# A hybrid block on one core: two weight sums of a pooling unit move to VectorE, its passes stand behind low parts, early branch weights, and the pooling weights' loads ahead of head 0's v

## The chip, the core and the metric

One core of one Trainium2 chip runs the whole kernel. The metric is the device time of one execution in microseconds (us). The kernel before takes 889.95 us, the median of three runs between 889.82 and 890.5. All times below are from one profiled execution of it, unless the text says otherwise.

## The reference, cut to what matters

One layer on 512 tokens of width 1024: a norm, one wide projection whose columns feed three mixers and the branch gates, the three branches merged by sigmoid gates, an output projection, and a feed-forward part. The change sits where the projection's pooling columns and the third branch's gate columns are computed, and where the pooling mixer and the first attention head begin.

```python
h = rms_norm(x, norm_mix[l])
proj = jnp.einsum('bsd,dc->bsc', h, w_in[l])
u_pool, u_lru, q, k, v, g_logits = jnp.split(proj, splits, axis=-1)
gates = jax.nn.sigmoid(g_logits + b_gate[l]).reshape(B, S, N_BRANCH, D_MODEL)
...
for g, w in enumerate(POOL_WINDOWS):            # windows 2, 4, 8, 16
    ug = u32[..., g * POOL_GROUP:(g + 1) * POOL_GROUP]
    cs = jnp.cumsum(ug, axis=1)
    cs_lag = jnp.pad(cs, ((0, 0), (w, 0), (0, 0)))[:, :S]
    outs.append((cs - cs_lag) / jnp.minimum(pos, float(w)) - ug)
y_pool = jnp.einsum('bsgi,gij->bsgj', jnp.stack(outs, axis=2), w_pool) * pool_scale
...
merged = (gates[:, :, 0] * jnp.einsum('bsc,cd->bsd', y_pool, w_branch[l, 0])
          + gates[:, :, 1] * jnp.einsum('bsc,cd->bsd', y_lru, w_branch[l, 1])
          + gates[:, :, 2] * jnp.einsum('bsc,cd->bsd', y_sb, w_branch[l, 2]))
```

## The kernel before, in words

Every product runs in float32 as three matmuls: each operand is split into a high part (rounded to fp32r) and a low part (the rest), and high by high, high by low and low by high are added in PSUM. `split_w` (L136) splits a weight tile of 128x1024: ScalarE writes the high part `whi` (L142), VectorE the low part `wlo` (L143). Both come from a pool of three buffers, so the split for product n+3 waits until TensorE is done with product n.

Q, k and v, the pooling columns and the gate columns of the third branch use a seven-product scheme: a square of four weight blocks 11, 12, 21, 22 is multiplied with seven products, named 11, 12, S1, S2, S3, S4, 22, whose weights are sums of blocks. The sums are built in place. A load on SyncE's queue brings a block, and a DMA on GpSimd's queue adds another block to it (`accum_op=ALU.add`, "an adding DMA" below), or VectorE adds two tiles. `pool_load` (L239) loads the pooling blocks and adds 22 to 21 (L244); `add_pool7` (L246) splits, and then starts the next sum with an adding DMA (L251). `seven_load` (L189) and `add_seven` (L200) do the same for the gate blocks (L196, L198), with two sums on VectorE (L207, L212) and one adding DMA (L213).

The stage concerned runs from 248.8 us on: 14 products for two pooling units in the order `PORDER` (L231), then 14 for two gate units (3 and 4) in `ORDER` or `UORDER`. Each product is 24 matmuls of 256 columns (`product`, L336, L342). The pooling units' PSUM tiles are `ps_uy`, `ps_ux`, the gate units' `ps_gy`, `ps_gx`. A product's half of a PSUM tile is used again by a later one, so ScalarE first copies it out: "a snap", L957 into `u` (pooling), L985 into `gx`, `gy` (gates). When a tile is complete, VectorE adds it to its snap (L962, L921). Then `pool_mean` (L927) makes the windowed mean of each half of `u` on VectorE: one pass per window, a running sum (L937) with a short one for the first columns (L936), or a shifted add (L934) for window 2, and two more operations (L939, L941). For the gates, `gate_done` (L919) takes the sigmoid (L923) and stores the tile to DRAM over GpSimd's queue (L925).

Behind the gates come head 0's transposes `pq` (L1102), the first branch product `ps_br` with the lru output loaded back as `yHH`, `yHL` over GpSimd's queue (L1250), the scores `z` of head 0 in three tiles from a pool of two PSUM buffers (`scores`, L1116), and the pooling map `pps` (`pool_back`, L1057). ScalarE reads `z` twice (L1135 writes `K`, L1136 writes `A`), which frees its PSUM buffer. The pooling weights `rawp` are loaded over SyncE's queue (L1045) and split by ScalarE (L1047, `wph`) and VectorE (L1048). `q_scales` (L842) makes the row scales of q on GpSimd, and its first operation is a power (L369).

The order of each engine's instructions is fixed when the kernel is built: a scheduler follows the program's order and the priorities (`high_priority`, `issue_after`). Each engine and each queue then works through its list in that order, and an instruction that waits holds up all behind it.

## Time and profile before

| | us |
|---|---|
| median of three runs | 889.95 |
| the profiled execution's own time | 890.54 |
| its span, first to last instruction | 888.8 |
| TensorE busy in the span | 863.5 |
| VectorE, ScalarE, GpSimd busy | 744.7, 528.2, 96.7 |

The profile is of one execution. Its page lists the busy time of each engine (PE is TensorE, DVE is VectorE, ACT is ScalarE, POOL is GpSimd, SP is SyncE). The view of waits says what TensorE stood idle for. The chain of waits follows the work that ended last. The table by stretch gives busy time, number of instructions, granted clock of TensorE (PEclk, 1.00 is full) and DMA share. A row of the timeline has start, duration, engine, line and tiles, and in brackets the idle time of the engine ahead of it with what ended it.

### The profile page before, as it was taken

To read this page: it belongs to the slowest core of one execution; us is meant where nothing else is said; L and a number is where in the kernel's file an instruction comes from. 1 tells how busy PE (TensorE), PEld (TensorE's weight loads), DVE (VectorE), ACT (ScalarE), POOL (GpSimd) and SP (SyncE) were. 2 spreads that over 40 slices of the span, in tenths; PEclk is the share of its full clock that TensorE was granted. 3 is DMA by queue.
4 is the path that set the end of the run, shared out by engine and by line. 5 is a ranking of instruction groups with operands and counts; after the bars stand their busy time and mean duration, and the time that the engine had idled before them with its cause. 6 is when DMAs were issued, how large, how long until landed. Compare 5 with 4: busy or idle time off the path is not lost.

```text
span 888.8 us, 14571 instructions
## 1 busy us (share of the span) xinstructions
PE 863.5 (97%) x5707; PEld 794.9 (89%) x5707; DVE 744.7 (84%) x947; ACT 528.2 (59%) x733; POOL 96.7 (11%) x139
## 2 busy tenths in 40 slices
PE   9999999999989896999999999999999999999998
PEld 7888878888879895888988998889999999999998
DVE  6899898979766964897998696699988898898974
ACT  7555998667844364676655554545555555754642
POOL 1010002232360021000000200000000000121200
PEclk9999999999999999999999999999999999999999
DMA  9685365997799358754554975437353343788923
GB/s 341 168 302 162 96 205 151 286 266 229 251 252 255 72 167 282 211 159 147 193 146 91 204 184 186 128 99 199 111 139 109 96 119 102 233 209 210 195 51 119
DMA packets 114757, 158.31 MB, mean 178 GB/s; under 512 B 8320, under 2 KB 86144, under 8 KB 114688
## 3 DMA queue, kind: packets, MB, share of 16 engines
q1 hardware_dynamic: 100864, 107.30, 38.0%
q0 software_dynamic: 13680, 49.81, 24.5%
q8 instruction: 45, 0.74, 0.4%
q10 hardware_dynamic: 144, 0.26, 0.1%
q14 instruction: 24, 0.20, 0.1%
HBM read 136.90 MB, written 18.87 MB: 175 GB/s over the span
## 4 chain that ended last, share of the span: by engine, by line
PE 80%; ACT 6%; DVE 6%; DMA 4%; issue 2%; POOL 1%; SPq 0%; DVEq 0%; ACTq 0%; POOLq 0%
PE ps_y L342 11%; PE ps_x L342 8%; PE ps_q L858 7%; PE ps_dy L1710 5%; PE ps_dx L1710 4%; PE ps_br L334 3%; PE ps_br L335 3%; PE ps_br L333 3%; PE ps_bY L1334 2%; PE ps_gate L761 2%; PE ps_gy L342 2%; DMA pw<-in_w_pool_dram 2%; PE ps_bX L1334 2%; DVE wlo L143 2%; ACT whi L142 1%
## 5 line engine op out<-in xcount | busy, mean ns | idle before, releaser
L142 ACT ACTIVATE whi<-raw 128x1024 fp32r<-128x1024 f32 x61 | 64.3, 1054 | 64.9 <-PE ps_out L334 15.3
L143 DVE TENSOR_TENSOR wlo<-raw,whi 128x1024 fp32r<-128x1024 f32 x61 | 74.3, 1220 | 15.9 <-ACT whi L142 15.5
L142 ACT ACTIVATE whi<-qw 128x1024 fp32r<-128x1024 f32 x48 | 50.4, 1053 | 33.8 <-PE ps_q L858 11.9
L143 DVE TENSOR_TENSOR wlo<-qw,whi 128x1024 fp32r<-128x1024 f32 x48 | 58.3, 1219 | 13.7 <-ACT whi L142 13.7
L1495 ACT ACTIVATE wh_S<-w_S 128x1024 fp32r<-128x1024 f32 x36 | 38.4, 1066 | 28.9 <-PE ps_y L342 20.3
L1616 POOL DMA_DIRECT2D dw<-in_w_down_dram x20 | 17.4, 971 | 306.1 <-DMA dw<-in_w_down_dram 253.6
L1496 DVE TENSOR_TENSOR wl_S<-w_S,wh_S 128x1024 fp32r<-128x1024 f32 x36 | 43.8, 1219 | 3.3 <-ACT wh_S L1495 3.3
L1495 ACT ACTIVATE wh<-w 128x1024 fp32r<-128x1024 f32 x27 | 28.7, 1063 | 27.5 <-PE ps_x L342 9.4
L1496 DVE TENSOR_TENSOR wl<-w,wh 128x1024 fp32r<-128x1024 f32 x27 | 32.9, 1219 | 7.8 <-ACT wh L1495 7.8
L1495 ACT ACTIVATE whdS<-dw 128x1024 fp32r<-128x1024 f32 x20 | 21.2, 1061 | 20.1 <-PE ps_dy L1710 10.6
L143 DVE TENSOR_TENSOR wlo<-pw,whi 128x1024 fp32r<-128x1024 f32 x14 | 17.1, 1221 | 16.5 <-ACT whi L142 16.4
L1496 DVE TENSOR_TENSOR wldS<-dw,whdS 128x1024 fp32r<-128x1024 f32 x20 | 24.1, 1219 | 4.9 <-ACT whdS L1495 4.9
L142 ACT ACTIVATE whi<-pw 128x1024 fp32r<-128x1024 f32 x14 | 14.8, 1059 | 21.9 <-DMA pw<-in_w_pool_dram 14.1
L1139 DVE TENSOR_TENSOR_SCAN E<-K,ahead 128x512 f32<-128x512 f32 (+3 forms) x32 | 25.3, 812 | 1.1 <-ACT K L1135 1.0
L333 PE MATMUL ps_br<-yHH,whi 128*128 128x512 f32 x64 | 25.2, 394 | 0.5 <-DVE gy L921 0.5
L334 PE MATMUL ps_br<-yHL,whi 128*128 128x512 f32 x64 | 25.2, 394 | 0.0
L335 PE MATMUL ps_br<-yHH,wlo 128*128 128x512 f32 x64 | 24.8, 387 | 0.0
L333 PE MATMUL ps_lru<-HH,whi 128*128 128x512 f32 x64 | 24.6, 384 | 0.0
L333 PE MATMUL ps_br<-yph,whi 128*128 128x512 f32 x64 | 24.5, 383 | 0.0
L333 PE MATMUL ps_gate<-HH,whi 128*128 128x512 f32 x64 | 24.4, 381 | 0.0
L335 PE MATMUL ps_lru<-HH,wlo 128*128 128x512 f32 x64 | 24.3, 379 | 0.0
L334 PE MATMUL ps_lru<-HL,whi 128*128 128x512 f32 x64 | 24.3, 379 | 0.0
(778 smaller groups left out, 3557.2 us busy)
## 6 DMA issues: line engine op xcount, KB each, us to landing
qw<-in_w_qkv_dram SPq DMA_DIRECT2D x24, 512.0 KB, 7.1
raw<-in_w_in_dram SPq DMA_DIRECT2D x23, 512.0 KB, 5.1
dw<-in_w_down_dram POOLq DMA_DIRECT2D x20, 512.0 KB, 8.6
w<-in_w_ffn_gate_dram SPq DMA_DIRECT2D x36, 256.0 KB, 4.1
w<-in_w_ffn_up_dram SPq DMA_DIRECT2D x36, 256.0 KB, 4.1
raw<-in_w_branch_dram SPq DMA_DIRECT2D x16, 512.0 KB, 4.1
qw<-in_w_qkv_dram POOLq DMA_DIRECT2D x12, 512.0 KB, 8.2
qd<-r POOLq DMA_DIRECT2D x12, 512.0 KB, 7.2
```

Of the source, the lines that this page charges most:

```text
L142: act(hi, raw, AF.Copy)
L143: los.append(dve.tensor_tensor(lo, raw, hi.bitcast(F32), ALU.subtract).ins)
L333: nc.tensor.matmul(ps, lh, rh, start=start, stop=False, skip_group_check=skip)
L334: nc.tensor.matmul(ps, lh, rl, start=False, stop=False, skip_group_check=skip)
L335: nc.tensor.matmul(ps, ll, rh, start=False, stop=stop, skip_group_check=skip)
L342: nc.tensor.matmul(o, a_[a][:, w, k, :], il2(b_[b][:, k, :]), start=first and n == k == 0, stop=last and n == 2 and k == 3, skip_group_che ...
L858: nc.tensor.matmul(ps[:, a, :], b_[:, k, ts_], il(a_[:, kk, :]), start=first and n == k == 0, stop=n == 2 and k == 3, skip_group_check=True)
L1139: dve.tensor_tensor_scan(E[:, c0:c0 + n][:, ::-1], K[:, c0 + 1:c0 + n + 1][:, ::-1], ahead[:, S - n:][:, ::-1], 0.0, ALU.mult, ALU.add)
L1334: nc.tensor.matmul(o, ah[x_][:, w, k, :], il2(b[k][y_]), start=first_ and n == k == 0, stop=n == 2 and k == 3, skip_group_check=True)
L1495: act(h, src, AF.Copy)
L1496: dve.tensor_tensor(l, src, h.bitcast(F32), ALU.subtract)
L1710: nc.tensor.matmul(o, a_[a][:, w, k0 + k, :], il2(b_[b][:, k, :]), start=first and i == k == 0, stop=last and i == 2 and k == nk - 1, skip ...
```

## The change

Six edits, all between the pooling units and head 0:

1. Pooling unit 0: the weights of S2 and S4 are sums made on VectorE, in place of two adding DMAs. One adding DMA (for S3) is left. Unit 1 keeps its three.
2. `PORDER` has another order.
3. `pool_mean` does one pass a call and is called behind given products (`MEAN` for unit 0, in gate unit 4 for unit 1), each pass placed behind the latest low part; it was one entry of the list of background work for two passes.
4. Gate unit 4 uses `ORDER` like unit 3 (S3 ahead of S4); `UORDER` is gone.
5. Three branch weight tiles are called for in gate unit 3 (`load_early`), and `q_scales` stands behind the last adding DMA of pooling unit 1.
6. The four `rawp` tiles are taken first and their loads stand ahead of head 0's v; the loads of head 0's q and k are called where its tasks are made.

```diff
     def add_direct(key, src, a, b):
-        def make(n):
+        def load(n):
             raw = wp.tile([P, a, b], F32, tag="raw", name="raw" + n)
             raws.append(nc.sync.dma_start(raw, src).ins)
-            return split_w(raw, [P, a, b], n)
+            return raw
+
+        def make(n):
+            return split_w(early.pop(key, None) or load(n), [P, a, b], n)
...
-    UORDER = {4: ("11", "12", "S2", "S1", "S4", "S3", "22")}
...
-    PORDER = ((0, "11"), (0, "S1"), (1, "11"), (1, "S1"), (0, "S2"), (0, "12"), (0, "S3"), (1, "S2"),
-              (0, "S4"), (0, "22"), (1, "12"), (1, "S3"), (1, "S4"), (1, "22"))
+    PORDER = ((0, "11"), (0, "S1"), (1, "11"), (0, "S2"), (0, "12"), (0, "S3"), (1, "S1"), (0, "S4"),
+              (0, "22"), (1, "S2"), (1, "12"), (1, "S3"), (1, "S4"), (1, "22"))
...
     def add_pool7(u, nm):
         def make(n):
-            parts = split_w(praw[u, {"S1": "21", "S2": "21", "S3": "11", "S4": "21"}.get(nm, nm)], [P, 2, 4, P], n)
-            if nm in PNEXT:
+            if u == 0 and nm == "S4":
+                r = praw[u, "12"]
+                dve.tensor_tensor(r, r, praw[u, "S2"], ALU.add)
+            buf = {"S1": "21", "S2": "21" if u else "S2", "S3": "11", "S4": "21" if u else "12"}.get(nm, nm)
+            parts = split_w(praw[u, buf], [P, 2, 4, P], n)
+            if u == 0 and nm == "S1":
+                praw[u, "S2"] = r = b4([2, 4, P], f"ps{u}")
+                dve.tensor_tensor(r, praw[u, "11"], praw[u, "21"], ALU.add)
+                state["s3"] = nc.gpsimd.dma_start(praw[u, "11"], pool_src(u, "21"), accum_op=ALU.add)
+            elif u and nm in PNEXT:
                 buf, m = PNEXT[nm]
-                nc.gpsimd.dma_start(praw[u, buf], pool_src(u, m), accum_op=ALU.add)
-            seven_load(3, {(1, "S2"): ("11",), (0, "S4"): ("21",), (0, "22"): ("12", "22")}.get((u, nm), ()))
+                state["acc"] = nc.gpsimd.dma_start(praw[u, buf], pool_src(u, m), accum_op=ALU.add).ins
+            seven_load(3, {(0, "S4"): ("11", "21"), (0, "22"): ("12", "22")}.get((u, nm), ()))
             return parts
...
-        def pool_mean(cc, j):
+        def pool_mean(cc, j, n):
             u2 = upool[cc, j]
-            p2 = b4([2, S], f"pw{cc}{j}")
-            for n in range(2):
+            if n == 0:
+                upool["p"] = b4([2, S], f"pw{cc}{j}")
+            p2 = upool["p"]
+            with tc.issue_after(los[-1]):
...
+        MEAN = ((0, "S4"), (0, "22"), (1, "S2"), (1, "12"))
...
-                bg.append(lambda cc=cc, j=j: pool_mean(cc, j))
+                means.extend([(cc, j, 0), (cc, j, 1)])
+            if (cc, nm) in MEAN:
+                pool_mean(*means.pop(0))
...
-                if (cc, nm) == (1, "12"):
-                    q_scales()
+                if (cc, nm) == (0, "12"):
+                    with tc.issue_after(state["acc"]):
+                        q_scales()
+                if cc == 0 and nm in ("S2", "S1", "S3"):
+                    load_early({"S2": ("br", 1, 0, 0), "S1": ("br", 1, 0, 1), "S3": ("br", 1, 1, 0)}[nm])
+                if cc and nm not in ("11", "22") and means:
+                    pool_mean(*means.pop(0))
...
         def load_pool_weights(g):
-            raw = slot_ld(f"rawp{g}", (2, 256))
+            raw = rawp[g]
...
+        for g in (2, 3, 0, 1):
+            rawp[g] = slot_ld(f"rawp{g}", (2, 256))
         tick(4)
         for h in range(2):
             for g in (2 * h, 2 * h + 1):
                 load_pool_weights(g)
+            if h:
+                head0()
```

How this moves the instructions, at three places. Up to pooling unit 0's first three products all engines' lists are the same.

**Place 1: the pooling units.** GpSimd's queue before; `pw011` is block 11 of unit 0, `pw121` block 21 of unit 1, `qw3210` block 21 of gate unit 3, `qd` the q store, `qrs` the row scales.

```order
L251 DMA pw011_2085<-in_w_pool7_dram 128x1024
L251 DMA pw021_2087<-in_w_pool7_dram 128x1024
L811 DMA qd01_85<-r010_2187 128x2x512
L251 DMA pw111_2169<-in_w_pool7_dram 128x1024
L369 TENSOR_TENSOR qrs_110<-qss_111,mhalf_82 128x32
...
L251 DMA pw121_2171<-in_w_pool7_dram 128x1024
L846 TENSOR_SCALAR qrs_110<-qrs_110 128x32
L251 DMA pw021_2087<-in_w_pool7_dram 128x1024
L251 DMA pw121_2171<-in_w_pool7_dram 128x1024
L198 DMA qw3210_2465<-in_w_gate7_dram 128x1024
L213 DMA qw3110_2435<-in_w_gate7_dram 128x1024
```

The same with the change.

```order
L265 DMA pw011_2085<-in_w_pool7_dram 128x1024
L828 DMA qd01_85<-r010_2187 128x2x512
L268 DMA pw111_2169<-in_w_pool7_dram 128x1024
L268 DMA pw121_2171<-in_w_pool7_dram 128x1024
L207 DMA qw3210_2434<-in_w_gate7_dram 128x1024
L268 DMA pw121_2171<-in_w_pool7_dram 128x1024
L386 TENSOR_TENSOR qrs_110<-qss_111,mhalf_82 128x32
...
L863 TENSOR_SCALAR qrs_110<-qrs_110 128x32
L222 DMA qw3110_2432<-in_w_gate7_dram 128x1024
```

The two sums into `pw021` are gone, the power stands behind all of unit 1's sums, and the gate block's sum `qw3210` stands ahead of unit 1's last one. ScalarE's list for unit 1 before (`whi76` is split for 12, `whi77` for S3, `whi78` for S4, `u10` the snap behind S2).

```order
L142 ACTIVATE whi76_2526<-pw112_2213 128x1024
L957 ACTIVATE u10_2339<-ps_uy1_2338 128x2x256
L142 ACTIVATE whi77_2564<-pw111_2169 128x1024
L142 ACTIVATE whi78_2602<-pw121_2171 128x1024
L142 ACTIVATE whi79_2630<-pw122_2215 128x1024
L142 ACTIVATE whi80_2659<-qw3110_2435 128x1024
L957 ACTIVATE u11_2371<-ps_uy1_2338 128x2x256
```

The same with the change.

```order
L142 ACTIVATE whi76_2532<-pw112_2213 128x1024
L142 ACTIVATE whi77_2565<-pw111_2169 128x1024
L142 ACTIVATE whi78_2599<-pw121_2171 128x1024
L977 ACTIVATE u10_2339<-ps_uy1_2338 128x2x256
L142 ACTIVATE whi79_2631<-pw122_2215 128x1024
L142 ACTIVATE whi80_2660<-qw3110_2432 128x1024
L977 ACTIVATE u11_2463<-ps_uy1_2338 128x2x256
```

The snap behind S2 now stands behind the split for S4, `whi78`, which reads the last sum.

**Place 2: the last gate unit.** VectorE's list before, from the low part of S4 (`wlo91`) to the one for the third branch tile.

```order
L143 TENSOR_TENSOR wlo91_3035<-qw4120_2709,whi91_3034 128x1024
L143 TENSOR_TENSOR wlo92_3064<-qw4110_2669,whi92_3063 128x1024
L143 TENSOR_TENSOR wlo93_3093<-qw4220_2753,whi93_3092 128x1024
L921 TENSOR_TENSOR gx1_2963<-gx1_2963,ps_gx1_2968 128x1024
L143 TENSOR_TENSOR wlo94_3127<-raw94_3124,whi94_3126 128x1024
L143 TENSOR_TENSOR wlo95_3158<-raw95_3155,whi95_3157 128x1024
L921 TENSOR_TENSOR gy1_2964<-gy1_2964,ps_gy1_2967 128x1024
L143 TENSOR_TENSOR wlo96_3448<-raw96_3445,whi96_3447 128x1024
```

With the change, from the low part of S3 (`wlo91`) to that of 22; `pw10`, `pw11` are the passes of pooling unit 1.

```order
L143 TENSOR_TENSOR wlo91_3028<-qw4110_2670,whi91_3027 128x1024
L955 SCALAR_TENSOR_TENSOR pw10_3022<-u10_2339,zero_117 128x16
L956 SCALAR_TENSOR_TENSOR pw10_3022<-u10_2339,pw10_3022 128x496
L958 SCALAR_TENSOR_TENSOR pw10_3022<-pw10_3022,invpos_112 128x15
L960 SCALAR_TENSOR_TENSOR u10_2339<-pw10_3022,u10_2339 128x512
L143 TENSOR_TENSOR wlo92_3062<-qw4120_2701,whi92_3061 128x1024
L955 SCALAR_TENSOR_TENSOR pw11_3090<-u11_2463,zero_117 128x8
L956 SCALAR_TENSOR_TENSOR pw11_3090<-u11_2463,pw11_3090 128x504
L958 SCALAR_TENSOR_TENSOR pw11_3090<-pw11_3090,invpos_112 128x7
L960 SCALAR_TENSOR_TENSOR u11_2463<-pw11_3090,u11_2463 128x512
L143 TENSOR_TENSOR wlo93_3096<-qw4220_2736,whi93_3095 128x1024
```

Four passes of four instructions each now stand between these low parts; before, they stood between those of gate unit 3. ScalarE's list before, at the unit's end (`gy1<-ps_gy1` is the snap behind S3, the rows from `gx1` with x2 the sigmoids).

```order
L985 ACTIVATE gx1_2963<-ps_gy1_2967 128x2x256
L142 ACTIVATE whi93_3092<-qw4220_2753 128x1024
L985 ACTIVATE gy1_2964<-ps_gx1_2968 128x2x256
L142 ACTIVATE whi94_3126<-raw94_3124 128x1024
L142 ACTIVATE whi95_3157<-raw95_3155 128x1024
L923 ACTIVATE gx1_2963<-gx1_2963,vt_72 128x512 x2
L985 ACTIVATE gy1_2964<-ps_gy1_2967 128x2x256
L142 ACTIVATE whi96_3447<-raw96_3445 128x1024
L923 ACTIVATE gy1_2964<-gy1_2964,vt_72 128x512 x2
```

The same with the change.

```order
L1007 ACTIVATE gx1_2959<-ps_gy1_2963 128x2x256
L142 ACTIVATE whi93_3095<-qw4220_2736 128x1024
L1007 ACTIVATE gy1_2960<-ps_gx1_2964 128x2x256
L142 ACTIVATE whi94_3128<-rawbr_1_0_0_2827 128x1024
L1007 ACTIVATE gy1_2960<-ps_gy1_2963 128x2x256
L142 ACTIVATE whi95_3160<-rawbr_1_0_1_2859 128x1024
L940 ACTIVATE gx1_2959<-gx1_2959,vt_72 128x512 x2
L142 ACTIVATE whi96_3448<-rawbr_1_1_0_2890 128x1024
L940 ACTIVATE gy1_2960<-gy1_2960,vt_72 128x512 x2
```

The snap behind S3 moved ahead of one split (`whi95`) and of the sigmoids.

**Place 3: head 0.** GpSimd's queue before, with the lru output's second half and the gate stores.

```order
L1250 DMA yHL1_3434<-ydl1_105 128x1024
L1250 DMA yHH1_3433<-ydh1_103 128x1024 x2
L925 DMA gd210_100<-gx1_2963 128x1024
L1250 DMA yHL1_3434<-ydl1_105 128x1024
L925 DMA gd211_101<-gy1_2964 128x1024
```

The same with the change.

```order
L1286 DMA yHL1_3437<-ydl1_105 128x1024
L1286 DMA yHH1_3436<-ydh1_103 128x1024
L942 DMA gd210_100<-gx1_2959 128x1024
L1286 DMA yHH1_3436<-ydh1_103 128x1024
L942 DMA gd211_101<-gy1_2960 128x1024
L1286 DMA yHL1_3437<-ydl1_105 128x1024
```

The last two `yH` loads now stand behind a gate store each, and so behind its sigmoid. ScalarE's list before, at head 0's first scores.

```order
L142 ACTIVATE whi97_3525<-raw97_3523 128x1024
L1135 ACTIVATE K0_3214<-z0_0_3351,qrs_110 128x512
L1047 ACTIVATE wph0_3249<-rawp0_3247 128x512
L1136 ACTIVATE A0_0_3355<-z0_0_3351,qrs_110 128x512
L1047 ACTIVATE wph1_3255<-rawp1_3253 128x512
L1135 ACTIVATE K1_3215<-z0_1_3411,qrs_110 128x128
L1136 ACTIVATE A0_1_3418<-z0_1_3411,qrs_110 128x128
```

The same with the change.

```order
L142 ACTIVATE whi97_3526<-raw97_3524 128x1024
L1076 ACTIVATE wph0_3254<-rawp0_3233 128x512
L1164 ACTIVATE K0_3217<-z0_0_3354,qrs_110 128x512
L1076 ACTIVATE wph1_3259<-rawp1_3234 128x512
L1165 ACTIVATE A0_0_3358<-z0_0_3354,qrs_110 128x512
L1040 ACTIVATE p00h_3263<-u00_2272 128x512
L1164 ACTIVATE K1_3218<-z0_1_3414,qrs_110 128x128
```

Both reads of `z0_0` now stand behind a split of pooling weights. On SyncE's queue one row moved: the load of head 0's v, `at02`, stands behind the four `rawp` loads and not ahead of them. The three branch tiles' loads stand at the same rows as before, under other names.

23 lines of the change are left out of this document (16 added, 7 removed).

## Prediction

> **What bounds the kernel.** The page first: TensorE is busy nearly the whole span, so an edit counts only where TensorE stands idle or runs slow.
>
> ```profile
> span 888.8 us, 14571 instructions
> PE 863.5 (97%) x5707; PEld 794.9 (89%) x5707; DVE 744.7 (84%) x947; ACT 528.2 (59%) x733; POOL 96.7 (11%) x139
> ```
>
> The view of waits says where it stands idle (total, times, longest, in us).
>
> ```profile
> PE z L333 <- ACT A L1136: 4.4, 1, 4.4
> PE ps_gy L342 <- ACT gy L985: 2.7, 1, 2.7
> PE ps_uy L342 <- ACT whi L142: 2.7, 1, 2.7
> PE ps_gy L342 <- ACT gx L985: 2.2, 2, 1.5
> PE ps_gx L342 <- DVE wlo L143: 1.5, 1, 1.5
> PE ps_br L333 <- DVE gy L921: 0.5, 1, 0.5
> ```
>
> All lie in the stretch that the change rewrites. The chain of waits gives an undisturbed product: 24 matmuls in 2.68 us.
>
> ```profile
> 277.10 2.68 PE ps_ux L342 x24
> ```
>
> The table by stretch gives what each stretch took (first figure), the engines' busy time, and as the third figure from the end the granted clock.
>
> ```profile
> 248.80:293.00 44.20, 39.89 (x337) 39.18 (x336) 27.20 (x34) 19.57 (x23) 16.93 (x18) 0.96 0.88 228
> 293.00:340.50 47.50, 40.50 (x346) 38.93 (x344) 37.01 (x46) 24.41 (x30) 6.97 (x13) 1.00 0.53 139
> 264.00:267.00 3.00, 3.00 (x15) 3.00 (x16) 2.45 (x2) 1.92 (x3) 0.90 (x1) 0.53 1.09 261
> 336.00:340.00 4.00, 3.80 (x32) 3.58 (x32) 0.74 (x1) 1.02 (x2) 1.03 (x2) 1.00 0.93 261
> 353.40:358.90 5.50, 5.50 (x15) 4.50 (x16) 4.09 (x8) 4.42 (x11) 0.00 (x0) 0.50 1.08 324
> ```
>
> Fourteen products are 14 x 2.68 = 37.5 us. So the pooling units lose 44.2 - 37.5 = **6.7 us**; the gate units, with 1.0 for the transposes, 47.5 - 38.5 = **9.0 us**; head 0 the 4.4 us wait for `A`, and behind it 5.5 us at half the clock, 5.5 x 0.50 = 2.75, together **7.15 us**. That is 22.9 us, the most that the edits could win.
>
> **The pooling units.** Before, ScalarE's splits wait for adding DMAs, and all behind them on ScalarE waits too, the snap `u` with it.
>
> ```profile
> 261.51 1.06 ACT L142 ACTIVATE whi<-pw 128x1024 fp32r<-128x1024 f32 x1 [5.17 <-DMA pw<-in_w_pool_dram]
> 269.88 1.06 ACT L142 ACTIVATE whi<-pw 128x1024 fp32r<-128x1024 f32 x1 [3.96 <-DMA pw<-in_w_pool_dram]
> 270.84 0.58 ACT L957 ACTIVATE u<-ps_uy 128x512 f32<-128x512 f32 x1
> ```
>
> The page's row of these low parts, and the landing times of the six adding DMAs of L251:
>
> ```profile
> L143 DVE TENSOR_TENSOR wlo<-pw,whi 128x1024 fp32r<-128x1024 f32 x14 | 17.1, 1221 | 16.5 <-ACT whi L142 16.4
> ```
>
> ```profile
> DMA to landing us min/median/max: 5.5/8.6/13.9
> ```
>
> The change removes two and adds two sums on VectorE of the low part's shape, 2 x 1.22 us; these hide, since VectorE is idle 16.5 us ahead of these low parts, and without that cover they would cost at most 2.4. The waits ahead of unit 0's S2 and S3 go: S2's weights are ready 1.2 us behind the first low part. What is late next is unit 1. Without waits its S3 starts 11 products behind 248.8, at 248.8 + 11 x 2.68 = **278.3**. It writes over what the snap behind S2 reads, and that snap now stands on ScalarE behind `whi78`, which needs the last sum into `pw121`. On GpSimd's queue that sum stands behind the gate block's sum, which waits for the plain load of `qw3210`.
>
> ```profile
> 275.81 0.86 POOL L198 DMA_DIRECT2D qw<-in_w_gate_dram x1 [2.45 <-DMA qw<-in_w_gate_dram]
> ```
>
> The power on GpSimd, and the landing times of the plain loads of L196:
>
> ```profile
> 253.13 6.66 POOL L369 TENSOR_TENSOR qrs<-qss,mhalf 128x32 f32<-128x32 f32 x1
> ```
>
> ```profile
> DMA to landing us min/median/max: 3.3/6.9/13.3
> ```
>
> Before, the gate block's sum waited for that load until just ahead of 275.8. Its buffer comes free earlier now, with the low part of unit 0's S3, about 261.5 by the products' pace; with the loads' spread it lands between 265 and 275. I take 272, nearer the upper end, since two loads of q and k stand ahead of it and adding DMAs keep the 16 engines full (share 1.09 above). The last sum is issued 0.9 us later and takes 8.6, the median, because it runs behind another: 281.5. Then `whi78` 1.06 and the snap 0.58 less overlap: S3 starts about 282.8, a stall of **4.5 us**. Bounds: the load at 268 and 5.5 us give no stall; 275.3 and 8.6 give 8. The power (6.66 us) that stood between the sums now follows them, and is wanted only at head 0.
>
> A stall of 4.4 us cost half the clock for 5.5 us above; a 2.7 us one did so ahead of 264 (0.53), and another did not ahead of 336 (1.00). I add 2.7, bounds 0 and 2.75. New loss 4.5 + 2.7 = 7.2 against 6.7: **+0.5 us**. The Trainium skill ("TensorE: Matmul & The Clock Gate", section "HAM oscillation — how this bites in real kernels") puts the limit at idle gaps over about 3.4 us: by it a stall of 4.5 cools and one of 3 does not. The trace agrees for 4.4; the 2.7 us wait that cooled was followed at once by one of 0.8.
>
> **The gate units.** VectorE's passes (first rows) fill its list ahead of a low part; ScalarE's snaps stand behind a split, and at the end behind the sigmoids.
>
> ```profile
> 300.09 1.26 DVE L937 TENSOR_TENSOR_SCAN pw<-u,pw 128x504 f32<-128x504 f32 x1
> 302.49 0.67 DVE L941 SCALAR_TENSOR_TENSOR u<-pw,u 128x512 f32<-128x512 f32 x1
> ```
>
> ```profile
> 302.88 1.06 ACT L142 ACTIVATE whi<-qw 128x1024 fp32r<-128x1024 f32 x1 [3.36 <-PE ps_gx L342]
> 303.84 0.58 ACT L985 ACTIVATE gx<-ps_gy 128x512 f32<-128x512 f32 x1
> 334.35 1.32 ACT L923 ACTIVATE gx<-gx,vt 128x512 f32<-128x512 f32 x2
> 335.57 0.57 ACT L985 ACTIVATE gy<-ps_gy 128x512 f32<-128x512 f32 x1
> ```
>
> The last `gy` sum on VectorE:
>
> ```profile
> 339.26 1.22 DVE L921 TENSOR_TENSOR gy<-gy,ps_gy 128x1024 f32<-128x1024 f32 x1 [3.42 <-PE ps_gy L342]
> ```
>
> With the change unit 3's snap stands one split earlier, unit 4's S3 comes one product ahead of S4, and its snap ahead of a split and of the sigmoids. Per product ScalarE then does a split and a snap, 1.06 + 0.58 = 1.64 of 2.68 us: about 1 us to spare. VectorE's four passes of unit 1 (1.26 + 0.67 + short ones, about 1.95 each) now stand between unit 4's low parts: 1.95 + 1.13 (the pace back to back) = 3.1 us per product against 2.68. The low parts run ahead by about 3 us, so none of unit 4 is late, but behind its last product VectorE is. Counted from unit 4's first product, S1's split waits for that product (2.7) and unit 3's second sigmoid pair (to about 3.3), and with its low part is done at 5.5; then follow four passes, five low parts and the `gx` sum in a row, 7.8 + 5.6 + 1.1 = 14.5, so the last `gy` sum runs from 20.0 to 21.3. TensorE is through its products and transposes at 7 x 2.68 + 1.0 = 19.8, and `ps_br`, whose PSUM that sum frees, waits 1.5 us and not 0.5. I leave 2.0 of the 9.0 (0.3 inside, 1.7 ahead of `ps_br` with the restart; bounds 0.8 and 4): **-7.0 us**.
>
> **Head 0.** The chain of waits ahead of the 4.4 us (`at` stands at SPq L1095):
>
> ```profile
> 342.14 6.30 DMA gd<-gy
> ...
> 348.57 0.37 SPq L1095
> ...
> 348.99 3.10 DMA rawp<-in_w_pool_dram
> ...
> 352.11 0.63 ACT wph L1047
> 352.74 0.59 ACT A L1136
> ```
>
> The landing times of the `yH` loads of L1250:
>
> ```profile
> DMA to landing us min/median/max: 4.1/8.0/9.6
> ```
>
> Before, the `rawp` loads stood behind head 0's v, whose buffer waited for the gate store of 6.30 us; `z` went on 12.9 us behind the last `gy` sum (340.5 to 353.4). Now they follow the third branch tile's load: one low part (1.2) and two issues (0.37 each in the chain) behind that sum, at 2.0 and not 8.5 us. But they share the engines with two gate stores and two `yH` loads, pushed later by place 3 of the change. The second one lands between 2.0 + 0.4 + 3.1 = 5.5 and the 12 us of before; I take 10.2, since the branch tiles ahead of it have to share too. The split and `A`, 0.63 + 0.59, follow: 11.4 us. TensorE needs a matmul of 512 columns every 2 x 2.68 / 24 = 0.22 us; by its list about 38 stand ahead of the first use of the last `yHL`, 8.3 us, and 4 more ahead of the third `z` tile. That `yHL` load goes out 2.0 us behind the sum (1.4 for the sigmoid, 0.6 for the store's issue) and lands 8.0 later, the median: 10.0, so 1.7 us of wait, bounds 0 and 3.3. TensorE is at `z` by 10.9 and waits 0.5 more: `z` goes on at 11.4 us, 1.5 less than before. The idle time falls into short pieces, so I expect the clock to stay: -2.75. The splits behind `z`, hidden under half the clock before, show 0.8: **-3.4 us**, bounds -7.15 and +2.
>
> The early calls of the branch tiles change names, not rows, on SyncE's list: nothing.
>
> **The sum.** 0.5 - 7.0 - 3.4 = -9.9 us. Against the profiled execution's own 890.5 that is 880.6; the median lies 0.6 lower, which is less than any bound here, and I say **881**.
>
> **Rivals.**
> - *Short stall.* The last sum lands by 278 or so: a stall of at most 1.5 us at full clock in the pooling units, 5.7 us less: **875**. For: two adding DMAs less in front; against: loads beside adding DMAs took up to 13.3. By the Trainium skill ("DMA: Bandwidth & Descriptors", section "Queues, rings and completion order") each engine takes turns between queues packet by packet, which would bring `qw3210` in by about 270; by it the time would be this rival's, near 876 as an estimate. The trace does not settle it: such loads took from 3.3 to 13.3 us, and no row here tells what each ran beside.
> - *Head 0 wins nothing.* `rawp` queues behind the branch tiles and everything that moved later, `z` waits as long as before and the clock halves again: 3.4 + 2 more: **886**.
> - *The wanted gain is only moved.* Stall of 8 us, cooling, and head 0 as before: 0.5 + 3.5 - 7 + 2 = -1: **889.5**, within 0.2%. It is the case in which the change does not do what it says.
> - *Slower.* The one mechanism: GpSimd's list holds unit 1's last sum behind the gate block's. Each us that `qw3210` lands later than 272 costs a us; the price eats the 9.9 when it lands behind 282, and gives **892** at 283.4. Against: 13.3 us was the longest of 32 such loads, and this would be over 20.
>
> **How the numbers follow.** Forecast 0.42, short stall 0.25, head 0 wins nothing 0.18, gain only moved 0.08, slower 0.07. The range runs from 873 (no stall, and 2 us of head 0's further bound) to 889, just short of the case without gain; between 0.15 and 0.2 is left out. A measurement here tells 0.2%, 1.8 us, from no change: faster 0.85, same 0.08, slower 0.07.
>
> **What would show it.** In the changed kernel's waits: no `ps_uy` wait for `whi` of S2; one wait of S3 of unit 1 for the `u` snap of 3 to 6 us, with PEclk near 0.5 behind it; no wait over 1 us of `ps_gx`, `ps_gy`; `ps_br` waiting 1 to 2 us for `gy`; `z` or `ps_br` waiting 1 to 3 us, with PEclk 1.00 behind. It is wrong if the unit 1 wait is absent or over 8, if gate waits stay, or if `z` waits 4 us again.

## The result, and the profile after

The changed kernel takes 879.97 us (median of nine runs, 877.51 to 886.13) against 889.69 before (nine runs). The ratio, taken from all runs and not from the two medians, is 0.9914, 95% interval 0.9887 to 0.9941, so it is 0.6 to 1.1% faster. The profiled execution took 886.13, the longest of the nine; a second profile (first experiment below) is of one that took 879.74. Line numbers have moved with the change: the gate and pooling products are now L359, the snaps L977 and L1007, the gate sums L938, the reads of `z` L1164 and L1165, the loads of `rawp` L1074.

The page of the changed kernel, then its view of waits (total, times, longest, in us):

```profile
span 884.3 us, 14573 instructions
PE 865.3 (98%) x5707; PEld 796.4 (90%) x5707; DVE 748.1 (85%) x949; ACT 527.8 (60%) x733; POOL 95.8 (11%) x137
```

```profile
PE ps_uy L359 <- ACT u L977: 2.8, 1, 2.8
PE z L350 <- ACT A L1165: 2.3, 1, 2.3
PE ps_br L351 <- DMA yHL<-ydl: 1.5, 1, 1.5
PE pq L1131 <- issue: 1.5, 1, 1.5
...
PE ps_br L350 <- DVE gy L938: 1.2, 1, 1.2
```

The waits of S2 for `whi` and of the gate products are gone. What is left is one wait in the pooling units and four at the end of the gates and in head 0. The same view of the second profile has the same waits with other lengths:

```profile
PE ps_br L351 <- DMA yHL<-ydl: 2.9, 1, 2.9
PE pq L1131 <- issue: 1.5, 1, 1.5
...
PE z L350 <- ACT A L1165: 1.3, 1, 1.3
PE ps_uy L359 <- ACT u L977: 1.2, 1, 1.2
PE ps_br L350 <- DVE gy L938: 1.2, 1, 1.2
```

The table by stretch, cut at the first pooling product, the first gate product, the first `ps_br` matmul and the restart of `z` (first figure the length, third from the end the granted clock), of the first profile and of the second:

```profile
249.24:291.48 42.24, 39.42 (x338) 39.22 (x337) 32.13 (x40) 19.47 (x23) 15.19 (x15) 0.96 0.86 215
291.48:332.84 41.36, 38.75 (x347) 38.35 (x345) 34.92 (x40) 24.64 (x30) 5.78 (x11) 1.00 0.56 149
332.84:347.68 14.84, 11.24 (x44) 8.98 (x44) 5.33 (x6) 5.71 (x10) 3.59 (x9) 0.85 0.99 321
```

```profile
249.11:288.13 39.02, 37.78 (x337) 37.59 (x336) 30.51 (x39) 19.56 (x23) 14.83 (x13) 1.00 0.87 229
288.13:329.49 41.36, 38.75 (x347) 38.35 (x345) 36.55 (x42) 24.65 (x30) 7.16 (x13) 1.00 0.60 151
329.49:344.27 14.78, 10.54 (x45) 8.37 (x45) 5.56 (x6) 5.94 (x11) 3.59 (x9) 0.87 1.00 317
```

Before, these stretches took 44.2, 47.5 and 12.9 us. The pooling units won 2.0 and 5.2 us, the gate units 6.1 in both profiles, and the stretch up to the restart of `z` lost 1.9. From the first `ps_br` matmul to the first product of head 0's output `py`, a stretch that holds the half clock behind `z` too, it is 43.8 and 42.4 us, and was 42.8 before. The two profiles differ most in the pooling units, and there in the clock: 0.96 against 1.00.

### The profile page after: what moved, and what is told of

Same layout as the page of the kernel before. It is cut to its first block, busy times and chain, and to the rows that moved or that the text cites. A ratio compares the mean times of both kernels' runs of the same rounds, so it can differ in the third digit from the quotient of the medians.

```text
span 884.3 us, 14573 instructions
## 1 busy us (share of the span) xinstructions
PE 865.3 (98%) x5707; PEld 796.4 (90%) x5707; DVE 748.1 (85%) x949; ACT 527.8 (60%) x733; POOL 95.8 (11%) x137
## 4 chain that ended last, share of the span: by engine, by line
PE 84%; DVE 5%; ACT 5%; DMA 4%; issue 1%; SPq 0%; ACTq 0%; DVEq 0%
PE ps_y L359 11%; PE ps_q L875 8%; PE ps_x L359 8%; PE ps_dy L1746 5%; PE ps_dx L1746 4%; PE ps_br L352 3%; PE ps_br L350 3%; PE ps_br L351 3%; PE ps_bY L1370 2%; PE ps_gy L359 2%; PE ps_bX L1370 2%; PE ps_gx L359 2%; PE ps_uy L359 2%; PE ps_gate L778 2%; DVE wlo L143 1%; PE ps_lru L350 1%
## 5 line engine op out<-in xcount | busy, mean ns | idle before, releaser
L142 ACT ACTIVATE whi<-raw 128x1024 fp32r<-128x1024 f32 x58 | 61.2, 1055 | 64.6 <-PE ps_br L351 16.8
L143 DVE TENSOR_TENSOR wlo<-raw,whi 128x1024 fp32r<-128x1024 f32 x58 | 70.7, 1220 | 18.2 <-ACT whi L142 17.7
L1532 DVE TENSOR_TENSOR wl_S<-w_S,wh_S 128x1024 fp32r<-128x1024 f32 x36 | 43.8, 1218 | 3.3 <-ACT wh_S L1531 3.3
L351 PE MATMUL ps_gate<-HL,whi 128*128 128x512 f32 x64 | 24.3, 379 | 0.0
```

The source lines that it names most:

```text
L142: act(hi, raw, AF.Copy)
L143: los.append(dve.tensor_tensor(lo, raw, hi.bitcast(F32), ALU.subtract).ins)
L351: nc.tensor.matmul(ps, lh, rl, start=False, stop=False, skip_group_check=skip)
L1532: dve.tensor_tensor(l, src, h.bitcast(F32), ALU.subtract)
```

## The experiments

Each kernel is the changed one with the edits named. The changed kernel ran again beside numbers 2, 3 and 4; the others are compared with it through their ratios to the kernel before, which ran beside each.

| kernel | median us | ratio to before, 95% interval |
|---|---|---|
| changed | 880.0 | 0.9914 (0.9887 to 0.9941) |
| 1 changed, again | 880.6 | 0.9908 (0.9881 to 0.9935) |
| 2 unit 1's S4 sum on VectorE | 878.6 | 0.9883 (0.9865 to 0.9902) |
| 3 two passes earlier | 878.4 | 0.9878 (0.9856 to 0.9899) |
| 4 without edit 6 | 882.4 | 0.9917 (0.9900 to 0.9934) |
| 5 without edit 3 | 886.0 | 0.9954 (0.9935 to 0.9972) |
| 6 without edit 4 | 878.9 | 0.9870 (0.9841 to 0.9898) |
| 7 lru loads ahead of the stores | 876.8 | 0.9854 (0.9824 to 0.9885) |
| 8 edits of 2 and 3 | 877.9 | 0.9863 (0.9839 to 0.9888) |
| 9 gate block's sum last | 882.4 | 0.9913 (0.9892 to 0.9934) |
| 10 without edits 1 and 2 | 884.5 | 0.9933 (0.9915 to 0.9951) |
| 11 edit of 7, without edit 4 | 877.9 | 0.9866 (0.9843 to 0.9888) |
| 12 edits of 2, 3 and 7 | 876.5 | 0.9846 (0.9827 to 0.9865) |

### The clock: the changed kernel again

No edit.

> The changed kernel unaltered, for a second profile on another chip. Its first profile (span 884.3) shows four dips of the granted clock, each a whole number of 3.41 us pieces (3.4, 3.4, 6.8 and 3.4 us), one of them at 807 us where both kernels wait 0.9 and 0.8 us and the kernel before kept full clock. Theory A, dips go by a grid of 3.41 us that doesn't start with the program: the same waits stand in this profile (2.8 us of S3 for u, about 2.6 us of pq and ps_br, 1.5 for yHL, 2.3 for A), but at least one dip is in another place or missing, and the times scatter over 877 to 886. Theory B, a dip follows from the length of a wait alone: the same four dips and a spread under 3 us.

The table by stretch at the dips of the first profile, then at the dip of the second one (the first and last microseconds of a profile, where the clock is also low, left aside), then at the two waits near 810 us of the kernel before:

```profile
281.77:285.18 3.41, 3.41 (x16) 3.41 (x17) 3.41 (x5) 0.83 (x1) 0.00 (x0) 0.50 0.49 144
332.97:336.38 3.41, 3.41 (x9) 2.66 (x10) 2.59 (x3) 2.39 (x4) 2.22 (x7) 0.50 0.93 294
346.63:353.45 6.82, 5.55 (x15) 4.55 (x16) 6.82 (x12) 6.82 (x16) 0.00 (x0) 0.50 1.17 314
807.42:810.83 3.41, 3.41 (x18) 3.41 (x17) 3.41 (x6) 2.54 (x5) 0.00 (x0) 0.50 0.54 167
```

```profile
340.60:347.40 6.80, 5.21 (x13) 3.85 (x14) 4.83 (x8) 5.49 (x12) 0.00 (x0) 0.50 1.16 328
```

```profile
807.00:814.00 7.00, 5.51 (x47) 5.13 (x46) 3.99 (x7) 3.63 (x6) 0.00 (x0) 1.00 0.76 254
```

Theory A holds. The same waits stand in both profiles, though not all of the same length, but three of the four dips are missing in the second. The pair of waits near 807 us (0.9 and 0.8 us) halved the clock in the first profile, and not in the second nor in the kernel before (0.7 and 0.8 us), nor in experiment 7 with 1.0 and 0.8 us. Each dip lasts one or two pieces of 3.41 us, and the distances between their starts in the first profile, 51.20, 13.66 and 460.79 us, are 15, 4 and 135 times 3.413. So a dip costs at most 3.41 x 0.50 = 1.7 us or twice that, and whether a wait brings one depends on where it falls in a piece. The Trainium skill ("TensorE: Matmul & The Clock Gate", section "Part 1: The HAM clock gate (the "warmup" mystery)") says that the clock is decided in a free-running window of 3413 ns that doesn't start anew with the kernel; the traces agree with these distances.

The stall of S3 of unit 1 shows about where the line lies. It was 2.8, 2.7, 2.6, 2.4 and 2.0 us in the profiles of the changed kernel and of experiments 4, 6, 7 and 11, each with a dip behind it, and 2.0, 1.7, 1.6 and 1.2 in those of 5, 9, 3 and 1, without one.

The length of the wait is not what sorts these cases best; the busy time of TensorE in a piece is. Cut the fourteen profiles of this document along the grid that their own dips give, their first and last 20 us left aside. Of the pieces at full clock, all 24 with at most 1.48 us of busy time have a piece at half clock behind them, none with 1.9 us or more has, and of nine in between, two have. The kernel before then settles the two waits of 2.7 us that the prediction set side by side: the first falls into one piece (0.49 us busy, the second figure of its row; the clock halves), the second is cut by an edge (1.80 and 2.28; it doesn't). The last row is the piece ahead of the dip at 807 us in the changed kernel, one of the two in between.

```profile
259.98:263.39 3.41, 0.49 (x2) 0.30 (x2) 0.79 (x1) 1.88 (x3) 2.11 (x6) 1.00 1.06 293
331.66:335.07 3.41, 1.80 (x17) 1.61 (x15) 2.73 (x3) 2.74 (x4) 1.60 (x3) 1.00 0.38 101
335.07:338.48 3.41, 2.28 (x20) 2.28 (x21) 0.76 (x1) 1.08 (x2) 1.06 (x2) 1.00 0.88 209
```

```profile
804.01:807.42 3.41, 1.70 (x13) 1.32 (x12) 1.92 (x3) 3.01 (x5) 0.00 (x0) 1.00 0.38 148
```

### The pooling units

Experiment 9 makes the gate block's sum wait for unit 1's last one:

```diff
-                if nm == "21":
+                if nm == "21" and n != 3:
...
+            if (u, nm) == (1, "S2"):
+                with tc.issue_after(state["acc"]):
+                    nc.gpsimd.dma_start(qraw[3, "21", 0], seven_src(3, "22", 0), accum_op=ALU.add)
```

> The changed kernel with the gate block's sum qw3210 behind unit 1's last sum on GpSimd's queue. The prediction's theory (the last sum is held up by the gate block's sum and the load that this waits for): the stall ahead of unit 1's S3 goes. Rival, from the changed kernel's trace, where the gate block's sum was issued at 267.6 us and the last sum only at 272.4, when VectorE's low part for S2 was done: the buffer of the sums in place holds it up, so it is still issued behind that low part, at most 2 us sooner by what the two sums take from each other, and a stall of 0.5 to 3 us stays. The time is within 2 us of the changed kernel.

GpSimd's timeline of the changed kernel, then of this one (start, duration, engine, line, and in brackets the idle time and what ended it):

```profile
267.56 0.85 POOL L207 DMA_DIRECT2D qw<-in_w_gate_dram  x1 [4.02 <-DMA qw<-in_w_gate_dram]
272.44 0.85 POOL L268 DMA_DIRECT2D pw<-in_w_pool_dram  x1 [4.03 <-DVE wlo L143]
```

```profile
272.86 0.85 POOL L268 DMA_DIRECT2D pw<-in_w_pool_dram  x1 [9.89 <-DVE wlo L143]
```

In the changed kernel the gate block's sum goes out at 267.6, and the queue then stands idle for 4 us until VectorE's low part lets unit 1's last sum into `pw121`. With the gate block's sum out of the way the last sum is still released by that low part, at 272.9, and S3 waits 1.7 us, between the 2.8 and 1.2 of the two profiles. The queue didn't hold it up, and here the theory of the prediction falls. The gate block's sum may still slow the other one beside it: unit 1's last sum took 5.5 us from issue to landing here, 7.6 and 7.0 in the changed kernel. The time of the whole kernel says less, because the gate block's sum is late in turn: VectorE waits 3.8 us for it, and TensorE 1.6 us for the low part behind.

ScalarE's timeline of the changed kernel shows what does. The splits for S2 and S4 both read block 21 of unit 1, each after a sum into it:

```profile
269.82 1.06 ACT L142 ACTIVATE whi<-pw 128x1024 fp32r<-128x1024 f32 x1 [2.87 <-DMA pw<-in_w_pool_dram]
...
280.11 1.06 ACT L142 ACTIVATE whi<-pw 128x1024 fp32r<-128x1024 f32 x1 [5.59 <-DMA pw<-in_w_pool_dram]
281.08 0.58 ACT L977 ACTIVATE u<-ps_uy 128x512 f32<-128x512 f32 x1
```

It is a chain in one buffer: sum, split for S2, low part, next sum at 272.4, split for S4 at 280.1, snap, and S3 at 281.7. Experiment 2 cuts it: unit 1's S4 weights are block 12 plus the S2 weights, on VectorE, as in unit 0.

```diff
-            if u == 0 and nm == "S4":
+            if nm == "S4":
                 r = praw[u, "12"]
-                dve.tensor_tensor(r, r, praw[u, "S2"], ALU.add)
+                dve.tensor_tensor(r, r, praw[u, "21" if u else "S2"], ALU.add)
...
-            elif u and nm in PNEXT:
+            elif u and nm in ("11", "S1"):
```

> Unit 1's weights for S4 are a sum on VectorE too, so the last adding DMA into block 21 of unit 1 is gone. Both theories of the stall ahead of unit 1's S3 (held up on GpSimd's queue, or held up by the buffer that is added into in place) expect it to go: the wait of 2.8 us for u goes, and the half clock behind it (1.7 us). 4.5 us less than the changed kernel where its stall cools the clock, 2.8 where not. Rival: VectorE's 1.2 us more or the next load is late in its place, and the stretch of the pooling units stays at 42.2 us.

No wait for `u` is left, and the pooling units take 38.0 us by the starts of their first product and of the gates' (42.2 and 39.0 in the changed kernel), at full clock. VectorE isn't free of it: a wait for a low part has come into the first gate unit:

```profile
PE ps_gx L359 <- DVE wlo L143: 1.1, 1, 1.1
```

So the stall goes, and part of it comes back in the next stage: the gate units take 42.9 us and not 41.4, both stretches together 80.9 against 83.6 and 80.4. The median is 1.9 us lower than that of the changed kernel beside it, 878.6 against 880.6, with intervals that overlap.

Experiment 10 takes edits 1 and 2 back (the old `PORDER` and the adding DMAs; the last two of unit 0's four passes follow the two products that now stand behind its own):

```diff
-            if u == 0 and nm == "S4":
-                r = praw[u, "12"]
-                dve.tensor_tensor(r, r, praw[u, "S2"], ALU.add)
...
-            elif u and nm in PNEXT:
+            if nm in PNEXT:
...
-        MEAN = ((0, "S4"), (0, "22"), (1, "S2"), (1, "12"))
+        MEAN = ((0, "S4"), (0, "22"), (1, "12"), (1, "S3"))
```

> The changed kernel with the pooling units' sums and order as before (edits 1 and 2 undone). The prediction has edits 1 and 2 at +0.5 us, so this would be 0.5 us faster. Rival, by the two profiles of the changed kernel, where the pooling units took 42.2 and 39.0 us against 44.2: 2 to 5 us slower, with the waits of S2 for whi (2.7 us) and S3 for u (0.8) back, unless head 0's loads, which come at their own time, swallow the difference; then within 1 us.

Its waits in the pooling units:

```profile
PE ps_uy L352 <- ACT whi L142: 1.9, 1, 1.9
...
PE ps_uy L352 <- DVE wlo L143: 0.7, 1, 0.7
```

The old waits are back, and the clock dips behind them, for 6.8 us. The ratio is 0.9933 against 0.9914 and 0.9908: the two edits won about 2 us. The forecast had them at a loss of 0.5. The intervals overlap, so the size is no better known than that.

### The gate units

Experiment 5 puts the passes back on the list of background work, without the place behind the latest low part:

```diff
-                means.extend([(cc, j, 0), (cc, j, 1)])
+                bg.append(lambda cc=cc, j=j: (pool_mean(cc, j, 0), pool_mean(cc, j, 1)))
...
-            with tc.issue_after(los[-1]):
+            if 1:
```

> The changed kernel with edit 3 undone: the passes of the means go back to the list of background work, two a call, free to stand ahead of a low part. The prediction's step (low parts behind passes make the waits of the first gate unit, 1.6, 1.7 and 0.8 us before): those waits come back, about 4 us, while the last sums come out of VectorE earlier and pq and ps_br get back 2.1 of their 2.6 us. In all 2 us slower than the changed kernel. Rival: the order of the products in edit 4 took the waits away, not the passes; then this kernel is 2 us faster than the changed one.

```profile
PE ps_gx L359 <- DVE wlo L143: 4.4, 2, 3.4
```

Low parts behind passes are back, with 4.4 us in two waits; the waits of `pq` and `ps_br` shrink from 2.6 to 0.4 in its trace, which is of the fastest of its twelve runs. At 0.9954 against 0.9914 and 0.9908 it is about 4 us slower, with intervals that just overlap: of the edits taken back one at a time, edit 3 is worth the most.

Experiment 6 has S4 ahead of S3 in gate unit 4 again:

```diff
...
-            for nm in ORDER:
+            for nm in ((ORDER, ("11", "12", "S2", "S1", "S4", "S3", "22"))[cc]):
```

> The changed kernel with edit 4 undone: gate unit 4 has S4 ahead of S3 again. The prediction's step: the snap behind S3 stands behind two splits and the sigmoids again, so the last product waits for it, 2.9 us as before, or more, since VectorE's gx sum ahead of the sigmoids is later now; 2 to 4 us slower than the changed kernel. Rival: with the passes moved, the sigmoids come too late to stand ahead of the snap, and the time is within 1 us.

Its waits, and its table by stretch for the pooling and gate units together and for what follows up to the first product of head 0's output `py`:

```profile
PE ps_gy L359 <- ACT gy L1007: 3.1, 1, 3.1
PE ps_uy L359 <- ACT u L977: 2.6, 1, 2.6
PE ps_gy L359 <- DVE wlo L143: 1.5, 1, 1.5
```

```profile
249.22:337.88 88.66, 81.39 (x682) 80.58 (x680) 67.19 (x80) 44.31 (x54) 23.97 (x28) 0.94 0.72 192
337.88:375.00 37.12, 36.29 (x180) 29.71 (x180) 30.47 (x45) 27.31 (x50) 2.58 (x7) 1.00 0.81 240
```

The wait of the kernel before (2.7 us) is back as expected, 3.1 us long, with another of 1.5 ahead of it and a dip of 6.8 us; the pooling and gate units together take 88.7 us; the changed kernel took 83.6 and 80.4. Yet the kernel is no slower: its ratio of 0.9870 lies 3 to 4 us below those of the changed kernel, with intervals that just overlap. Neither `ps_br` nor `z` waits for a load, and the stretch to `py` takes 37.1 us at full clock, where the changed kernel took 43.8 and 42.4 by the same two starts. What edit 4 wins in the gates is lost in head 0; by these traces, because head 0 then starts ahead of its loads. So edit 4 alone is worth nothing here, and may cost time.

Experiment 3 moves two of unit 1's passes into gate unit 3 and puts the other two early in unit 4:

```diff
-                if cc and nm not in ("11", "22") and means:
+                if (cc, nm) in ((0, "S4"), (0, "22"), (1, "12"), (1, "S2")) and means:
```

> Two of unit 1's four passes go to gate unit 3, two stay in gate unit 4, both early in it. If VectorE's list of low parts and passes in gate unit 4 is what makes the last two sums late, the waits of pq (1.5 us) and ps_br (1.2 us) shrink to 0.5 in sum, and 2 us are won, or 3.7 where the clock had dipped behind them. Rival: the waits of the first gate unit come back (a low part behind passes, 1.5 us) and nothing is won; or the gate's end is earlier but z waits for the pooling weights as before and the gain is lost there.

VectorE's timeline of the changed kernel at the end of the gates, and this kernel's wait that is left:

```profile
327.56 0.69 DVE L960 SCALAR_TENSOR_TENSOR u<-pw,u 128x512 f32<-128x512 f32 x1
328.17 1.22 DVE L143 TENSOR_TENSOR wlo<-rawbr,whi 128x1024 fp32r<-128x1024 f32 x1
329.30 1.21 DVE L938 TENSOR_TENSOR gx<-gx,ps_gx 128x1024 f32<-128x1024 f32 x1
330.43 1.22 DVE L143 TENSOR_TENSOR wlo<-rawbr,whi 128x1024 fp32r<-128x1024 f32 x1
331.57 1.21 DVE L938 TENSOR_TENSOR gy<-gy,ps_gy 128x1024 f32<-128x1024 f32 x1
```

```profile
PE ps_br L350 <- DVE gy L938: 0.4, 1, 0.4
```

In the changed kernel VectorE comes from the last pass straight into low parts and sums without idle time. Both sums are late: `pq` starts at 330.6, when the `gx` sum ends, and `ps_br` when the `gy` sum does. With the passes earlier, the wait of `pq` is gone and that of `ps_br` falls to 0.4. The median is 2.2 us below the changed kernel's in the same set, with overlapping intervals.

### Head 0

Experiment 4 takes edit 6 back:

```diff
-            raw = rawp[g]
+            raw = slot_ld(f"rawp{g}", (2, 256))
...
-        head0 = abg[0]
+        abg[0]()
         abg[0] = nothing
-        for g in (2, 3, 0, 1):
-            rawp[g] = slot_ld(f"rawp{g}", (2, 256))
```

> The changed kernel with edit 6 undone: the pooling weights' loads stand behind head 0's v again. The prediction's step: z waits as it did before and the clock halves: 3.4 us slower than the changed kernel. Rival, by the changed kernel's trace, where z went on 15.1 us behind the first ps_br product and not 12.8 as before: the loads land late in either place since they share the engines with stores and loads, so the time is within 1 us.

The chain of waits of the changed kernel, then of this one:

```profile
334.18 0.37 SPq L149
...
334.60 10.93 DMA rawp<-in_w_pool_dram
...
347.27 0.59 ACT A L1165
```

```profile
334.64 0.98 SPq L1124
...
335.67 10.93 DMA rawp<-in_w_pool_dram
...
347.25 0.59 ACT A L1165
```

Head 0's v (L1124) goes out at 334.6, right behind the branch tile's load, and doesn't wait for the gate store that ended at 348.44 in the kernel before. Edit 6 therefore moves the `rawp` loads by one load, 1.1 us, and `z` doesn't start sooner, as ScalarE's list takes the 1.1 us back. Without edit 6, ScalarE writes `K` at 341.9, before the loads are in, and does one split of `rawp` ahead of `A`; with it, `K` and two splits stand between the first landing and `A`. The wait that edit 6 was to take away wasn't there any more once the other edits were in: the load of v no longer stands behind that store. Which edit brought this wasn't tried. The median is 1.8 us above that of the changed kernel beside it, but the ratios, 0.9917 and 0.9908, differ by less than their intervals, so a small gain of edit 6 stays open; 3.4 us is more than the trace has room for.

In both chains a load of 256 KB takes 10.9 us. In the changed kernel the share of the DMA engines in this stretch is 0.99, and 321 GB/s move. Experiment 7 asks what stands ahead of it:

```diff
-                    nc.gpsimd.dma_start(t[:, 2 * k2:2 * k2 + 2, :], d[i][:, 2 * k2:2 * k2 + 2, :])
+                    with tc.high_priority(600):
+                        nc.gpsimd.dma_start(t[:, 2 * k2:2 * k2 + 2, :], d[i][:, 2 * k2:2 * k2 + 2, :])
```

> The changed kernel with all four loads of the lru output's second half ahead of both gate stores on GpSimd's queue (in the changed kernel one stands behind each store). If head 0 is late because these loads go out late and then share the engines with the stores, the branch tiles and the pooling weights, the wait of ps_br for yHL (1.5 and 2.9 us in two profiles) goes, the pooling weights land 1 to 3 us earlier and z restarts 2 to 4 us earlier: 2 to 4 us faster. Rival: the engines are full in that stretch, and what is put first only pushes the pooling weights back: the wait for yHL goes, the wait of z for A grows by as much, and the time is within 1 us.

Its longest wait in head 0, and the load in its chain:

```profile
PE pps L350 <- ACT p00h L1040: 1.9, 1, 1.9
```

```profile
334.55 8.70 DMA rawp<-in_w_pool_dram
```

No wait for `yHL`, none of `z` for `A`; the `rawp` load takes 8.7 us and not 10.9. A wait of 1.9 us is left, of the pooling map for its split, which stands behind `rawp` too. At 876.8 (0.9854, runs from 874.69 to 880.52) this order is 4 to 5 us faster than the changed kernel's, more than any other edit tried here; its interval ends at 0.9885, where those of the changed kernel begin (0.9887 and 0.9881).

Experiment 11 adds to it the order of products of before:

> All loads of the lru output ahead of the gate stores, as in the seventh experiment, and edit 4 undone. Without edit 4 alone the time was that of the changed kernel: the gate units took 5 us more and head 0 took 7 less. If edit 4's gain was swallowed in head 0 because the loads come at their own time, it counts once they come early: 3 to 5 us slower than the seventh experiment (876.8). Rival: edit 4 is worth nothing in either setting, since the half clock and not the loads made the difference: within 1 us of it.

Its edits are those of experiments 6 and 7. The wait for the `gy` snap is there (3.1 us), and the pooling and gate units take 86.3 us against 83.2 in experiment 7, by the same starts; but the way to `py` is 39.1 and not 41.0, and the median 877.9 and not 876.8. The expectation of 3 to 5 us falls: even with the loads first, most of what edit 4 wins is waiting time in head 0 (1.9 of 3.1 us by these traces; the ratios don't tell the two kernels apart).

### Together

Experiment 8 has the edits of 2 and 3, experiment 12 those of 2, 3 and 7.

> The edits of the second and third experiment together: unit 1's S4 weights by VectorE, and two passes earlier. If both gains are independent: the stall ahead of unit 1's S3 and 2 us of the waits of pq and ps_br are gone, 2 to 3 us below the changed kernel's median and with a smaller spread, as there are fewer waits to cool the clock. Rival: VectorE has no room for both (the second experiment already had a wait of 1.1 us for a low part), and the time is no better than with one alone.

> Unit 1's S4 sum on VectorE, two passes earlier and all lru loads first. By the sum of the parts: 1 to 2 us below the changed kernel for the stall ahead of S3, 1 to 2 for pq and ps_br, 3 to 4 for head 0: 873 to 875. Rival: with the gate units done 3 us sooner, head 0's loads are late again and the time stays at 876 to 877.

Experiment 8 came to 877.9. The stall of S3 is gone, but these runs can't tell it from experiment 3 alone (0.9863 and 0.9878). Experiment 12 has the lowest median, 876.5, with runs from 875.75 to 876.91, but can't be told from experiment 7 alone. The rival has it: the sum of the parts would have been 873 to 875. Its view of waits shows where the rest went:

```profile
PE pps L350 <- ACT p00h L1040: 3.5, 1, 3.5
...
PE ps_gx L359 <- DVE wlo L143: 1.3, 2, 1.1
```

`ps_br` starts at 329.0 and not at 332.0 as in experiment 7, and the pooling map waits 3.5 us for its split behind `rawp` and not 1.9. Of the 3.0 us won in front, 1.9 are lost again up to `py` (42.9 us and not 41.0), where head 0 waits for its loads. What it may buy is the narrow spread of its four runs. That few waits are left that could halve the clock would explain it, and its trace has one dip of 3.4 us, but this wasn't shown.

## Why the prediction was right, and where it was wrong

The forecast was 881, the median is 880.0, and all fifteen runs of the changed kernel lie between 877.5 and 886.9, inside the range. The time came out right by luck in good part, because two terms are wrong in opposite directions. In the second profile the terms are -5.2, -6.1 and, by the stretch to `py`, -0.4 where the forecast has +0.5, -7.0 and -3.4; in the first they are -2.0, -6.1 and +1.0. The spans moved by -10.8 and -4.5 us, and -9.9 was forecast.

- **The pooling units, +0.5 forecast, -2.0 and -5.2 measured.** The stall of S3 behind the snap and `whi78` is where the prediction put it, 2.8 and 1.2 us and not 4.5. The step that failed is "On GpSimd's queue that sum stands behind the gate block's sum, which waits for the plain load of `qw3210`": that load was in by 267.6 and not 272, the last sum was not issued later for the gate block's, and it waited for the low part of S2 out of its own buffer (experiment 9). The 272 leaned on a mixed row: of the 32 loads that took 3.3 to 13.3 us, 24 are q, k and v weights of an earlier stage, and the eight gate loads took 3.3 to 8.7; the one in question took 7.0. That the last sum landed near 280 and 278, close to the 281.5 assumed, is luck: it was issued at 272.4 and 271.3, near the 272.9 assumed, but for another reason. The half clock behind it costs 1.7 us when it comes, not 2.7, and came in one of two profiles.
- **The rule on queues.** By the Trainium skill ("DMA: Bandwidth & Descriptors", section "Queues, rings and completion order") the load was to be in by about 270, and the time that of the short stall, 876. It was in by 267.6, so on the load the rule was nearer than the forecast. A short stall followed in one profile only, since the load wasn't what the last sum waited for; its case lay 4 us below the median.
- **The sums on VectorE.** They cost nothing that shows: unit 0 has no wait for them.
- **The gate units, -7.0 forecast, -6.1 measured in both profiles.** No gate product waits any more. At the end the `ps_br` wait of 1.2 us is near the 1.5 of the forecast; what it missed is that `pq` waits for the `gx` sum first, 1.5 us. Experiment 5 gives most of this gain to the passes. Experiments 6 and 11 show that little, if any, of edit 4's share reaches the end of the kernel.
- **Head 0, -3.4 forecast, +1.0 and -0.4 measured up to `py`.** Up to the restart of `z` the forecast had -1.5, and +1.9 was measured. The failed step is the landing of the second `rawp` load, "I take 10.2": it landed at 346.3, 13.5 us behind the end of the last `gy` sum (332.8), and the first at 345.5. The loads went out at 1.8 us, near the 2.0 of the forecast, and took 10.9 us where the first one had taken 3.1 before. The engines were fuller than before: a share of 0.99 against 0.87 up to the restart of `z`, as two gate stores, two `yH` loads, two branch tiles and four `rawp` loads go out within 6 us; experiment 7, with the `yH` loads ahead, has 8.7 us. Which of the others counts for how much wasn't tried. With it the half clock stayed, 6.8 us long in both profiles, where the prediction's sign was full clock behind this wait. The wait for `yHL`, 1.7 forecast, was 1.5 and 2.9. The mechanism is that of the rival "head 0 wins nothing"; its time of 886 didn't come about because the pooling units gave what head 0 didn't.
- **The idle limit.** The prediction weighed a limit of about 3.4 us of idle time (the Trainium skill, "TensorE: Matmul & The Clock Gate", section "HAM oscillation — how this bites in real kernels"). The traces go lower: waits of 2.0 to 2.8 us brought a dip, and so did 0.9 and 0.8 close together; what sorts the cases is the busy time within a piece of the grid.
- **The edits one by one.** Taken back singly, edit 3 is worth about 4 us, edits 1 and 2 about 2, edit 6 by the ratios less than 1, and edit 4 nothing or less than nothing. This doesn't add up to the whole gain (8 us by the ratios, 9 to 10 by the medians), so part of it belongs to edits together or to edit 5, which the prediction has at nothing and which no run separates.

## What to carry to other kernels

When a stage is made faster, look at which loads of the next stage are tied to its end and which come at their own time. Here 6 us won in the gates met loads that did not come sooner, and ordering those loads was worth as much as the largest edit. A sum built in place by DMAs is a chain through its buffer; its length is read from the rows of the splits and low parts between the sums, not from the queue. And where short waits are left, one profile isn't enough: the same wait can cost nothing or 1.7 us of half clock, by where it falls on the clock's grid, and the same program met that grid at another place in each of its two profiles.

## What was not expected of the hardware

The granted clock falls in pieces of 3.41 us on a grid of its own, and a single wait of 2.0 us can be enough. In these profiles the clock halved behind every piece in which TensorE was busy for at most 1.48 us, and behind none with 1.9 or more. In two profiles of the same program four dips and one, with stalls of 2.8 and 1.2 us, went with spans of 884.3 and 878.0 us.
